# Gate and up projections with stationary weights in the four feed-forward blocks of a two-layer trunk

## Chip, cores and metric

The kernel runs on one core of a Trainium2 chip. The metric is the device time of one execution in microseconds (us). Before the change three runs took 990.55, 991.48 and 993.41 us; their median is 991.48 us.

## What is computed

The input is one sequence of 256 tokens with 1024 features, in float32. Two layers follow. Each layer has three residual steps, and each step ends in a layer norm: a feed-forward block (FFN), a mixer, and a second FFN. The mixer of layer 0 is attention beside a gated unit, that of layer 1 a matrix memory. Here is the part that the change touches:

```python
D_MODEL = 1024; SEQ = 256; D_FF = 2816

def swiglu(x, w_gu, w_down):
    g, u = jnp.split(x @ w_gu, 2, axis=-1)
    return (jax.nn.silu(g) * u) @ w_down

for l in range(DEPTH):
    x = layer_norm(ALPHA * x + 0.5 * swiglu(x, ffn_w_gu[l, 0], ffn_w_down[l, 0]), ...)
    ...  # mixer of the layer, then layer_norm
    x = layer_norm(ALPHA * x + 0.5 * swiglu(x, ffn_w_gu[l, 1], ffn_w_down[l, 1]), ...)
```

So there are four FFNs, each with a gate/up weight of 1024 x 5632 and a down weight of 2816 x 1024.

## The kernel before

**Numbers in two halves.** Every float32 operand of a large product is split into a high part (a cast to fp32r on ScalarE, line 92) and a rest (a subtraction on VectorE, line 93). A product is then three matmuls, `mm3` at lines 119 to 122: high by high, high by low, low by high, all added up in one PSUM tile.

**Weights.** All weights lie in one DRAM tensor `W` of pages of 128 x 1024 floats (512 KB), in the order of use. A page passes through three rings: raw (6 buffers, the DMA's target, `w_dma`, line 73), then `whi` and `wlo` (9 buffers each, written by `w_split`, line 78). When the last matmul on page n has been written down, `w_done(n)` (line 86) splits page n + 9 and loads page n + 15. The split of page n + 9 writes the buffers of page n, so it waits for the matmuls that read page n.

**x transposed.** `xTh` and `xTl` hold the two halves of x with the features on the partitions, 8 blocks of 128 features by 256 tokens. Each layer norm rewrites them, one half of the tokens (t = 0, 1) after the other.

**Two ways to project.** `proj` (line 241) keeps 128 tokens of x stationary and streams weights: four pages, eight blocks of features, three matmuls each, so 24 matmuls with a moving operand of 512 columns. Its output has tokens on the partitions. `proj_t` (line 255) keeps 128 x 128 weights stationary and streams x: one page, eight blocks, 24 matmuls with a moving operand of 256 columns (all tokens). Its output has features on the partitions, that is, it comes out transposed. Before the change only the mixers use `proj_t`, for 4 pages in layer 0 and 8 in layer 1.

**The FFN** (`ffn`, line 310). The 2816 hidden features are 11 groups of 256. One group takes four pages, in which 256 columns of gate stand beside 256 columns of up. For each group and each t, `proj` fills one PSUM bank (`bank_m`, 3 buffers) with gate in its first half and up in its second. Then `post` (line 313) does silu of the gate on ScalarE (line 315), times up on VectorE (line 316), two TensorE transposes into the bank `ps_t` (line 320), and a split of the result into the two halves of `hT` (lines 92 and 93). That is 22 such steps in an FFN and 88 in all. The down projection (`out_proj`, line 265) takes `hT` as its stationary operand, 22 blocks of 128 hidden features.

**What sets the order.** `post` is a generator. `tick()` (line 107), called between pieces of a projection, advances it, so that its transposes stand in the source some 18 matmuls after the projection that it belongs to. Line 36 has a manual schedule for SyncE (the queue of DMA issues) alone. On TensorE, ScalarE, VectorE and GpSimd the order of the source is a priority: the scheduler that lays out the program may put a later instruction first where the earlier one is not ready by its reckoning. The order on each engine is then fixed, and engines wait for one another by semaphores.

Of the kernel before, what the change touches and what calls it, by code (L numbers as in the profile page):

```python
# [7 lines left out]
F32 = mybir.dt.float32  # L8
F32R = mybir.dt.float32r
BF = mybir.dt.bfloat16  # L10
AF = mybir.ActivationFunctionType
OP = mybir.AluOpType
AX = mybir.AxisListType

P = 128
S = 256
# [3 lines left out]
FG = 11  # L20
FC = 22
# [9 lines left out]
def trunk(ctx, tc, W, xT_d, x_d, g_d, b_d, rope_d, id_d, idb_d, mk_d, tri_d, sel_d,  # L31
          sg_d, sb_d, sw_d, sbt_d, cw_d, wif_d, bif_d, hg_d, out_d):
    nc = tc.nc
# [5 lines left out]
    pages = ctx.enter_context(tc.tile_pool(name="pages", bufs=PAGES))  # L39
# [11 lines left out]
    def bank_m(shape=(P, 512)):  # L51
        return bank("m", 3, shape)

    def bank_t(shape=(P, 512)):
        return bank("t", 1, shape)

    def page(name, shape, dt=F32):
        n = 1
        for d in shape[1:]:
            n *= d  # L60
        v = pages.tile([P, 516], dt, tag="p2", name=name, bufs=PAGES)[:, 0:n]
        if len(shape) == 3:
            v = v.rearrange("p (a b) -> p a b", a=shape[1])
        elif len(shape) == 4:
            v = v.rearrange("p (a b c) -> p a b c", a=shape[1], b=shape[2])
        return v
# [24 lines left out]
    def split(src, hi, lo):  # L91
        nc.scalar.copy(out=hi, in_=src)  # L92
        nc.vector.tensor_tensor(out=lo, in0=src, in1=hi.bitcast(F32), op=OP.subtract)  # L93
# [3 lines left out]
    def spawn(gen):  # L97
        side.append([0, gen])
        return gen
# [13 lines left out]
    def finish(gen):  # L113
        for e in list(side):
            if e[1] is gen:
                while e in side:
                    step(e)
# [51 lines left out]
    for c in range(4):  # L169
        if c == 0:  # L170
# [3 lines left out]
            for i in range(2):  # L174
                w = slice(i * 512, (i + 1) * 512)
# [14 lines left out]
    def load_consts():  # L190
        nc.sync.dma_start(out=identb, in_=idb_d)
        nc.sync.dma_start(out=maskb, in_=mk_d)
        nc.sync.dma_start(out=tri, in_=tri_d)
        nc.sync.dma_start(out=sel, in_=sel_d)
        nc.sync.dma_start(out=cw, in_=cw_d)
        nc.sync.dma_start(out=bif, in_=bif_d)
# [44 lines left out]
    def proj(t, n0, release, out=None, js=range(4)):  # L241
        ps = out if out is not None else bank_m()
        for j in js:
            rh = whi[n0 + j].rearrange("p (a n) -> p a n", a=2)
            rl = wlo[n0 + j].rearrange("p (a n) -> p a n", a=2)
            for i in range(2):
                kc = 2 * j + i
                mm3(ps, xTh[:, kc, t * P:(t + 1) * P], xTl[:, kc, t * P:(t + 1) * P],
                    rh[:, i, :], rl[:, i, :], kc == 0, kc == 7)
            if release:  # L250
                w_done(n0 + j)
            tick()
        return ps
# [55 lines left out]

    def ffn(n0, k, ln_prev, last=False):  # L310
        hT = {}

        def post(g, t, ps):
            hp = pages.tile([P, 2, 256], F32, tag="h", name="hp", bufs=3)
            nc.scalar.activation(out=hp[:, 0, :], in_=ps[:, 0:256], func=AF.Silu)  # L315
            nc.vector.tensor_tensor(out=hp[:, 1, :], in0=hp[:, 0, :], in1=ps[:, 256:512], op=OP.mult)  # L316
            yield 2
            pt = bank_t((P, 2, P))
            for c in range(2):
                nc.tensor.transpose(pt[:, c, :], hp[:, 1, c * P:(c + 1) * P], ident)  # L320
            q = page("hT", [P, 2, 2, P], F32R)
            hT[g, t] = q
            split(pt, q[:, 0], q[:, 1])

        if ln_prev is None:
            load_consts()
        order = [(0, 0), (1, 0), (0, 1), (1, 1)] + [(g, t) for g in range(2, FG) for t in range(2)]
        gens = []
        if ln_prev is None:
            order = [(g, t) for g in range(1, FG) for t in range(2)]  # L330
            ps = [bank_m(), bank_m()]
            for j in range(4):
                proj(0, n0, False, ps[0], (j,))
                proj(1, n0, True, ps[1], (j,))
            for t in range(2):
                gens.append(spawn(post(0, t, ps[t])))
        for g, t in order:
            if (g, t) == (0, 1) and ln_prev is not None:
                finish(ln_prev)
            ps = proj(t, n0 + 4 * g, t == 1)  # L340
            gens.append(spawn(post(g, t, ps)))

        def lhs(c, t):
            if (c // 2, t) not in hT:
                for e in gens:
                    finish(e)
            q = hT[c // 2, t]
            return q[:, 0, c % 2, :], q[:, 1, c % 2, :]

        return out_proj(FC, n0 + 4 * FG, lhs, 7, k, 2.0 * ALPHA, 4.0 * EPS, last)  # L350

    def mixer_ab(n0, k, ln_prev):
# [173 lines left out]
    def mixer_c(n0, k, ln_prev):  # L526
# [196 lines left out]
        return out_proj(8, n0 + 24, lhs, 8, k, ALPHA, EPS, False)  # L723

    ln = ffn(0, 0, None)
    ln = mixer_ab(66, 1, ln)
    ln = ffn(94, 2, ln)
    ln = ffn(160, 3, ln)
    ln = mixer_c(226, 4, ln)
    ln = ffn(258, 5, ln, True)  # L730
# [3 lines left out]
def _arrays(np, i):  # L734
    f32 = np.float32
    import ml_dtypes
    c = np.ascontiguousarray
    parts = []

    def ffn(l, f):  # L740
        gu = i["ffn_w_gu"][l, f].reshape(4, 2, P, 2, FG, 256).transpose(4, 0, 2, 1, 3, 5)
        parts.append(gu.reshape(44, P, 1024))
        parts.append(i["ffn_w_down"][l, f].reshape(FC, P, 1024))

    def cols(w):
        g = w.shape[1] // 512
        return w.reshape(4, 2, P, g, 512).transpose(3, 0, 2, 1, 4).reshape(4 * g, P, 1024)

    def chunks(w):
        n = w.shape[1] // P  # L750
        return w.reshape(8, P, n, P).transpose(2, 1, 0, 3).reshape(n, P, 1024)

    ffn(0, 0)
    ab = i["ab_w_in"][0]
    parts.append(cols(ab[:, 0:1536]))
    parts.append(cols(ab[:, 2048:2560]))
    parts.append(chunks(ab[:, 1536:2048]))
    parts.append(i["ab_w_out"][0].reshape(8, P, 1024))
    ffn(0, 1)
    ffn(1, 0)  # L760
    cw = i["c_w_in"][0]
    parts.append(cols(cw[:, 2048:3072]))
    qk = [h + 4 * j for h in range(4) for j in range(2)]
    cqk, co_ = chunks(cw[:, 0:1024])[qk], cols(cw[:, 1024:2048])
    for g in range(2):
        parts.append(cqk[4 * g:4 * g + 4])
        parts.append(co_[4 * g:4 * g + 4])
    parts.append(i["c_w_out"][0].reshape(8, P, 1024))
    ffn(1, 1)
    a = {}  # L770
    a["W"] = np.concatenate(parts, axis=0)
    x = i["x"][0]
    a["xT"] = c(x.T.reshape(8, P, S).transpose(1, 0, 2))
    a["x"] = c(x.reshape(2, P, D).transpose(1, 0, 2))
    a["g"] = i["ln_g"].reshape(6, D)
    a["b"] = i["ln_b"].reshape(6, D)
    inv = (10000.0 ** (-(np.arange(32, dtype=f32) / f32(32)).astype(np.float64))).astype(f32)
    ang = (np.arange(S, dtype=f32)[:, None] * inv[None, :]).astype(np.float64)
    co, si = np.cos(ang), np.sin(ang)
    cs = np.concatenate([co, co], axis=1)  # L780
    sn = np.concatenate([-si, si], axis=1)
    r = np.stack([cs / 8, sn / 8, cs, sn], axis=1).astype(f32)
    a["rope"] = c(r.reshape(2, P, 4, 64).transpose(1, 0, 2, 3))
    a["id"] = np.eye(P, dtype=f32)
    a["idb"] = np.eye(P).astype(ml_dtypes.bfloat16)
    m = np.where(np.arange(P)[None, :] > np.arange(P)[:, None], -1e30, 0.0)
    a["mk"] = np.stack([m, m.T], axis=1).astype(ml_dtypes.bfloat16)
    a["tri"] = (np.arange(S)[None, :] >= np.arange(P)[:, None]).astype(f32)
    sel = np.zeros((P, 4, P), f32)
    for h in range(4):  # L790
        sel[h, h, :] = sel[32 + h, h, :] = -1.0
    a["sel"] = sel
    a["sg"] = i["sgu_ln_g"]
    a["sb"] = i["sgu_ln_b"]
    a["sw"] = c(i["sgu_w"][0].transpose(2, 0, 1))
    a["sbt"] = c(np.repeat(i["sgu_b"][0].reshape(4, 2, 1, P), 64, axis=2).reshape(4, P, P).transpose(1, 0, 2))
    cv = np.concatenate([i["c_conv_w"][0], i["c_conv_b"]], axis=0).reshape(5, 8, P)[:, qk]
    a["cw"] = c(cv.transpose(2, 1, 0))
    a["wif"] = c(cw[:, 3072:3080].reshape(8, P, 8).transpose(1, 0, 2).reshape(P, 64))
    a["bif"] = np.concatenate([i["c_b_i"], i["c_b_f"]], axis=1).reshape(8, 1)  # L800
    a["hg"] = i["c_head_g"]
    return a
# [23 lines left out]
```

## Time and profile before

| | |
|---|---|
| three runs, us | 990.55, 991.48, 993.41 |
| span of the profiled execution, first to last instruction | 987.7 us |
| TensorE (PE) busy | 974.8 us, 99% |
| weight loads (PEld) busy | 788.2 us, 80% |
| VectorE (DVE) busy | 599.0 us, 61% |
| ScalarE (ACT) busy | 463.2 us, 47% |
| mean granted TensorE clock | 0.999 |
| DMA, over the span | 185 GB/s mean, 330 GB/s in the first 25 us |

The profile gives the span of the one profiled execution; its own time is not listed beside those of the three runs. From the span to the median run there are 3.8 us, which lie before the first and after the last instruction or in the difference between executions.

In the rows below a time at the start of a line is that of the first instruction of the row, in us from the start of the span, and the next number is how long it was busy. "out<-in" are the program's names. For a matmul the first name after the arrow is the operand that streams, the second the stationary one, and the last number of the shape is the count of columns streamed. Matmuls overlap, so what a matmul costs is read from the distance between two starts, not from its duration.

### The profile page before, as it was taken

To read this page: it belongs to the slowest core of one execution; us is meant where nothing else is said; L and a number is where in the kernel's file an instruction comes from. 1 tells how busy PE (TensorE), PEld (TensorE's weight loads), DVE (VectorE), ACT (ScalarE), POOL (GpSimd) and SP (SyncE) were. 2 spreads that over 40 slices of the span, in tenths; PEclk is the share of its full clock that TensorE was granted. 3 is DMA by queue.
4 is the path that set the end of the run, shared out by engine and by line. 5 is a ranking of instruction groups with operands and counts; after the bars stand their busy time and mean duration, and the time that the engine had idled before them with its cause. 6 is when DMAs were issued, how large, how long until landed. Compare 5 with 4: busy or idle time off the path is not lost.

```text
span 987.7 us, 12215 instructions
## 1 busy us (share of the span) xinstructions
PE 974.8 (99%) x4584; PEld 788.2 (80%) x4584; DVE 599.0 (61%) x822; ACT 463.2 (47%) x664; POOL 25.3 (3%) x36
## 2 busy tenths in 40 slices
PE   8999999999999999999999999999999999999997
PEld 5888888887888888888888888888888788888886
DVE  6565554586768555554765555448767885555534
ACT  5454443346645444443354444324675444444420
POOL 0000000020100000000000000001000000000000
PEclk9999999999999999999999999999999999999999
DMA  8874465485336555555564455656633365555511
GB/s 330 296 270 171 171 213 192 132 284 180 117 124 232 193 187 186 196 186 188 177 217 172 170 173 190 213 172 213 214 125 123 133 216 207 184 196 182 192 43 43
DMA packets 52202, 182.81 MB, mean 185 GB/s; under 512 B 6192, under 2 KB 6832, under 8 KB 52016
## 3 DMA queue, kind: packets, MB, share of 16 engines
q1 hardware_dynamic: 52144, 182.04, 53.8%
q8 instruction: 36, 0.59, 0.2%
q14 instruction: 22, 0.18, 0.1%
HBM read 180.97 MB, written 1.05 MB: 184 GB/s over the span
## 4 chain that ended last, share of the span: by engine, by line
PE 70%; DVE 2%; POOL 0%; issue 0%; ACT 0%; DVEq 0%
PE ps_m L120 15%; PE ps_m L121 15%; PE ps_m L122 15%; PE ps_a L120 8%; PE ps_a L121 8%; PE ps_a L122 7%; PE ps_t L320 1%; DVE wlo L93 1%; PE ps_a L232 1%; POOL hrs L201 0%; ACT whi L92 0%; PE ps_a L471 0%; DVE hst L652 0%; DVE num L679 0%; PE ps_a L633 0%
## 5 line engine op out<-in xcount | busy, mean ns | idle before, releaser
L93 DVE TENSOR_TENSOR wlo<-raw,whi 128x1024 fp32r<-128x1024 f32 (+1 forms) x325 | 394.1, 1221 | 188.2 <-ACT whi L92 184.6
L92 ACT CAST whi<-raw 128x1024 fp32r<-128x1024 f32 (+1 forms) x325 | 339.6, 1049 | 251.9 <-PE ps_a L122 146.1
L120 PE MATMUL ps_m<-whi,xTh 128*128 128x512 f32 x832 | 338.0, 407 | 1.5 <-ACT whi L92 1.5
L121 PE MATMUL ps_m<-wlo,xTh 128*128 128x512 f32 x832 | 330.0, 397 | 0.5 <-DVE wlo L93 0.5
L122 PE MATMUL ps_m<-whi,xTl 128*128 128x512 f32 x832 | 329.2, 396 | 0.0
L122 PEld LDWEIGHTS ps_m<-whi,xTl 128*128 128x128 f32 x832 | 156.4, 188 | 37.2
L120 PEld LDWEIGHTS ps_m<-whi,xTh 128*128 128x128 f32 x832 | 156.6, 188 | 35.6 <-ACT whi L92 2.7
L121 PEld LDWEIGHTS ps_m<-wlo,xTh 128*128 128x128 f32 x832 | 156.8, 188 | 34.1 <-DVE wlo L93 1.2
L120 PE MATMUL ps_a<-whi,hT 128*128 128x512 f32 (+1 forms) x352 | 138.6, 394 | 0.0
L121 PE MATMUL ps_a<-wlo,hT 128*128 128x512 f32 (+1 forms) x352 | 138.0, 392 | 0.0
L122 PE MATMUL ps_a<-whi,hT 128*128 128x512 f32 (+1 forms) x352 | 137.8, 392 | 0.0
L92 ACT CAST hT<-ps_t 128x256 fp32r<-128x256 f32 x88 | 32.5, 369 | 118.2 <-PE ps_t L320 118.2
L93 DVE TENSOR_TENSOR hT<-ps_t,hT 128x256 fp32r<-128x256 f32 x88 | 37.0, 421 | 79.2 <-ACT hT L92 79.2
L122 PEld LDWEIGHTS ps_a<-whi,hT 128*128 128x128 f32 x352 | 66.1, 188 | 15.3
L120 PEld LDWEIGHTS ps_a<-whi,hT 128*128 128x128 f32 x352 | 66.1, 188 | 15.0
L121 PEld LDWEIGHTS ps_a<-wlo,hT 128*128 128x128 f32 x352 | 66.2, 188 | 14.9
L316 DVE TENSOR_TENSOR hp<-hp,ps_m 128x256 f32<-128x256 f32 x88 | 36.8, 418 | 38.4 <-ACT hp L315 38.4
L315 ACT ACTIVATE hp<-ps_m 128x256 f32<-128x256 f32 x88 | 33.5, 381 | 54.3 <-PE ps_m L122 53.9
L210 DVE SCALAR_TENSOR_TENSOR xn<-xn,ps_a 128x512 f32<-128x512 f32 x24 | 16.0, 684 | 37.1 <-PE ps_a L122 37.0
L320 PEld LDWEIGHTS ps_t<-ident,hp 128*128 128x128 f32 x176 | 24.3, 139 | 11.9
L320 PE MATMUL ps_t<-ident,hp 128*128 128x128 f32 x176 | 33.4, 271 | 0.0
L201 POOL TENSOR_TENSOR lnrs<-lnrs,half 128x1 f32<-128x1 f32 x12 | 11.4, 951 | 821.1 <-DVE lnrs L200 793.7
(185 smaller groups left out, 589.6 us busy)
## 6 DMA issues: line engine op xcount, KB each, us to landing
raw<-in_W SPq DMA_DIRECT2D x323, 512.0 KB, 4.3
gb<-in_g SPq DMA_DIRECT2D x6, 512.0 KB, 3.9
gb<-in_b SPq DMA_DIRECT2D x6, 512.0 KB, 4.6
xn<-in_x SPq DMA_DIRECT2D x1, 1024.0 KB
out<-xn SPq DMA_DIRECT2D x4, 256.0 KB, 2.3
xt<-in_xT SPq DMA_DIRECT2D x3, 256.0 KB, 6.2
raw<-in_W SPq DMA_DIRECT2D x2, 256.0 KB, 3.4
swt<-in_sw SPq DMA_DIRECT2D x2, 256.0 KB, 6.4
```

Of the source, the lines that this page charges most:

```text
L92: nc.scalar.copy(out=hi, in_=src)
L93: nc.vector.tensor_tensor(out=lo, in0=src, in1=hi.bitcast(F32), op=OP.subtract)
L120: mm_(out=out, lhsT=lh, rhs=rh, start=start, stop=False)
L121: mm_(out=out, lhsT=lh, rhs=rl, start=False, stop=False)
L122: mm_(out=out, lhsT=ll, rhs=rh, start=False, stop=stop)
L201: nc.gpsimd.tensor_tensor(out=r, in0=r, in1=half[:, :width], op=OP.pow)
L210: nc.vector.scalar_tensor_tensor(out=sl, in0=sl, scalar=scale, in1=acc[i], op0=OP.mult, op1=OP.add)
L232: nc.tensor.transpose(pt[:, c, :], sl[:, c * P:(c + 1) * P], ident)
L315: nc.scalar.activation(out=hp[:, 0, :], in_=ps[:, 0:256], func=AF.Silu)
L316: nc.vector.tensor_tensor(out=hp[:, 1, :], in0=hp[:, 0, :], in1=ps[:, 256:512], op=OP.mult)
L320: nc.tensor.transpose(pt[:, c, :], hp[:, 1, c * P:(c + 1) * P], ident)
```

## The change

`ffn` gets a parameter `head`: 1 for the first FFN of the program, 2 for the other three. The first `head` groups of 256 hidden features are projected as before, with `proj` and `post`. The other hidden features are taken in chunks of 128 by a new function `chunk`: 20 chunks in the first FFN and 18 in each of the others, 74 in all. A chunk takes two pages, one of gate and one of up. `proj_t` of the gate page writes the first half of a bank, silu reads that half, `proj_t` of the up page writes the second half of the same bank, VectorE multiplies, and the product is split into `hT` from SBUF. There are no TensorE transposes in a chunk, and nothing in it is a generator: its instructions are written down at once. On the host the pages of the chunks are laid out as `proj_t` wants them. The number and size of the pages stay.

```diff
     def ffn(n0, k, ln_prev, last=False):
         hT = {}
+        head = 1 if ln_prev is None else 2
...
             q = page("hT", [P, 2, 2, P], F32R)
-            hT[g, t] = q
+            for c in range(2):
+                hT[2 * g + c, t] = (q[:, 0, c, :], q[:, 1, c, :])
             split(pt, q[:, 0], q[:, 1])
+
+        def chunk(c):
+            n = n0 + 4 * head + 2 * (c - 2 * head)
+            ps = bank_m()
+            hp = pages.tile([P, 2, 256], F32, tag="h", name="hp", bufs=3)
+            proj_t(n, ps[:, 0:256])
+            nc.scalar.activation(out=hp[:, 0, :], in_=ps[:, 0:256], func=AF.Silu)
+            proj_t(n + 1, ps[:, 256:512])
+            nc.vector.tensor_tensor(out=hp[:, 1, :], in0=hp[:, 0, :], in1=ps[:, 256:512], op=OP.mult)
+            q = page("hT", [P, 2, S], F32R)
+            split(hp[:, 1, :], q[:, 0], q[:, 1])
+            for t in range(2):
+                w = slice(t * P, (t + 1) * P)
+                hT[c, t] = (q[:, 0, w], q[:, 1, w])
...
-        order = [(0, 0), (1, 0), (0, 1), (1, 1)] + [(g, t) for g in range(2, FG) for t in range(2)]
         gens = []
         if ln_prev is None:
-            order = [(g, t) for g in range(1, FG) for t in range(2)]
+            order = []
...
+        else:
+            order = [(0, 0), (1, 0), (0, 1), (1, 1)]
         for g, t in order:
...
+        for c in range(2 * head, FC):
+            chunk(c)
 
         def lhs(c, t):
-            if (c // 2, t) not in hT:
+            if (c, t) not in hT:
                 for e in gens:
                     finish(e)
-            q = hT[c // 2, t]
-            return q[:, 0, c % 2, :], q[:, 1, c % 2, :]
+            return hT[c, t]
...
-    def ffn(l, f):
-        gu = i["ffn_w_gu"][l, f].reshape(4, 2, P, 2, FG, 256).transpose(4, 0, 2, 1, 3, 5)
-        parts.append(gu.reshape(44, P, 1024))
+    def ffn(l, f, head):
+        w = i["ffn_w_gu"][l, f]
+        gu = w.reshape(4, 2, P, 2, FG, 256).transpose(4, 0, 2, 1, 3, 5)
+        parts.append(gu[0:head].reshape(4 * head, P, 1024))
+        gc = w.reshape(8, P, 2, FC, P).transpose(3, 2, 1, 0, 4)
+        parts.append(gc[2 * head:].reshape(2 * (FC - 2 * head), P, 1024))
         parts.append(i["ffn_w_down"][l, f].reshape(FC, P, 1024))
...
```

## Rows read from the trace of the kernel before

**Rows 1.** The page, part 1: busy time, share of the span, instructions

```profile
PE 974.8 (99%) x4584; PEld 788.2 (80%) x4584; DVE 599.0 (61%) x822; ACT 463.2 (47%) x664; POOL 25.3 (3%) x36
```

**Rows 2.** PE's waits, longest in total: us in total, times, longest

```profile
PE ps_m L120 <- ACT whi L92: 1.5, 1, 1.5
PE ps_m L120 <- DVE qkc L619: 1.4, 1, 1.4
```

**Rows 3.** Groups of instructions: xcount | busy us, mean ns | idle before, releaser

```profile
L320 PE MATMUL ps_t<-ident,hp 128*128 128x128 f32 x176 | 33.4, 271 | 0.0
L92 ACT CAST whi<-raw 128x1024 fp32r<-128x1024 f32 x323 | 338.4, 1052 | 250.5 <-PE ps_a L122 146.1 <-PE ps_m L122 89.9 <-PE ps_m L121 8.6
L93 DVE TENSOR_TENSOR wlo<-raw,whi 128x1024 fp32r<-128x1024 f32 x323 | 392.8, 1224 | 186.6 <-ACT whi L92 183.1 <-DMA raw<-in_W 0.2
L315 ACT ACTIVATE hp<-ps_m 128x256 f32<-128x256 f32 x88 | 33.5, 381 | 54.3 <-PE ps_m L122 53.9
L316 DVE TENSOR_TENSOR hp<-hp,ps_m 128x256 f32<-128x256 f32 x88 | 36.8, 418 | 38.4 <-ACT hp L315 38.4
L92 ACT CAST hT<-ps_t 128x256 fp32r<-128x256 f32 x88 | 32.5, 369 | 118.2 <-PE ps_t L320 118.2
L93 DVE TENSOR_TENSOR hT<-ps_t,hT 128x256 fp32r<-128x256 f32 x88 | 37.0, 421 | 79.2 <-ACT hT L92 79.2
```

**Rows 4.** Timeline of PE, first FFN, one projection to the next

```profile
93.87 0.48 PE L120 MATMUL ps_m<-whi,xTh 128*128 128x512 f32 x1
94.19 0.40 PE L121 MATMUL ps_m<-wlo,xTh 128*128 128x512 f32 x1
...
99.56 0.38 PE L320 MATMUL ps_t<-ident,hp 128*128 128x128 f32 x2
99.69 0.48 PE L120 MATMUL ps_m<-whi,xTh 128*128 128x512 f32 x1
```

**Rows 5.** Timeline of PE, mixer of layer 0: matmuls of proj_t

```profile
265.84 0.28 PE L121 MATMUL ps_m<-xTl,whi 128*128 128x256 f32 x1
...
268.67 0.28 PE L121 MATMUL ps_m<-xTl,whi 128*128 128x256 f32 x1
...
270.24 0.28 PE L121 MATMUL ps_m<-xTl,whi 128*128 128x256 f32 x1
...
273.98 0.39 PE L120 MATMUL ps_a<-whi,cah 128*128 128x512 f32 x1
```

**Rows 6.** Timelines of PE and ACT, mixer of layer 1: one bank, two column ranges

```profile
723.68 0.23 PE L603 MATMUL ps_a<-maskb,identb 128*128 128x128 bf16 x1
...
723.87 0.23 PE L603 MATMUL ps_a<-maskb,identb 128*128 128x128 bf16 x1
...
724.14 0.47 ACT L606 ACTIVATE pT<-ps_a,cnat 128x256 f32<-128x256 f32 x1 [1.09 <-PE ps_a L603]
```

**Rows 7.** Timelines of PE and ACT, first FFN: end of a projection to its silu

```profile
101.17 0.40 PE L120 MATMUL ps_m<-whi,xTh 128*128 128x512 f32 x1
...
101.37 1.05 ACT L92 CAST whi<-raw 128x1024 fp32r<-128x1024 f32 x1 [0.30 <-PE ps_m L122]
102.33 0.38 ACT L315 ACTIVATE hp<-ps_m 128x256 f32<-128x256 f32 x1
```

**Rows 8.** Timeline of PE, mixer of layer 1: gates beside proj_t

```profile
707.59 0.28 PE L122 MATMUL ps_m<-xTh,wlo 128*128 128x256 f32 x1
707.79 0.28 PE L553 MATMUL ps_a<-ident,ifr 8*128 8x8 f32 x2
...
708.23 0.28 PE L121 MATMUL ps_m<-xTl,whi 128*128 128x256 f32 x1
...
713.24 0.28 PE L122 MATMUL ps_m<-xTh,wlo 128*128 128x256 f32 x1
713.81 0.60 PE L564 MATMUL ps_a<-tri,gnl 128*4 128x256 f32 x2 [0.29 <-DVE gnl L560]
```

**Rows 9.** Timeline of PE, mixer of layer 0: attention beside proj_t

```profile
261.59 0.36 PE L121 MATMUL ps_m<-xTl,whi 128*128 128x256 f32 x1
...
262.26 0.28 PE L120 MATMUL ps_m<-xTh,whi 128*128 128x256 f32 x1
262.51 0.66 PE L447 MATMUL ps_a<-ptp,vs 128*64 128x128 f32 x8
```

More of the change, by code (lines that the diff above doesn't have):

```diff
@@ L751, in chunks @@
         return w.reshape(8, P, n, P).transpose(2, 1, 0, 3).reshape(n, P, 1024)
-    ffn(0, 0)
+    ffn(0, 0, 1)
     ab = i["ab_w_in"][0]
@@ L758, in _arrays @@
     parts.append(i["ab_w_out"][0].reshape(8, P, 1024))
-    ffn(0, 1)
-    ffn(1, 0)
+    ffn(0, 1, 2)
+    ffn(1, 0, 2)
     cw = i["c_w_in"][0]
@@ L768, in _arrays @@
     parts.append(i["c_w_out"][0].reshape(8, P, 1024))
-    ffn(1, 1)
+    ffn(1, 1, 2)
     a = {}
```

## Prediction

> **What bounds the kernel now.** I read the page's first part first: TensorE (PE) is busy for 974.8 of 987.7 us, with the other engines at 61% and less [rows 1]. Then PE's own waits: the two longest are 1.5 and 1.4 us, in an execution of almost a millisecond [rows 2]. So time goes down only if PE gets less to do, and up whenever PE is made to wait. Last I read PE's timeline, because matmuls overlap and their cost is the distance between starts. In the FFN, one projection of 24 matmuls and the two transposes that come with it take 5.82 us, from 93.87 to 99.69 [rows 4]. Within it the 23 matmuls from 94.19 to 99.56 stand 233.5 ns apart [rows 4].
>
> **What is removed.** 24 x 0.2335 us are 5.60 us, so two transposes cost 5.82 - 5.60 = 0.22 us of PE. (Their durations say 271 ns each [rows 3]; overlap makes that useless here.) Before there are 88 such pairs. The first FFN keeps 2 and the others 4 each, so 74 go: 74 x 0.216 = **16.0 us less**.
>
> **What is exchanged.** 74 x 24 = 1776 matmuls of 512 columns become 3552 of 256 columns. The mixers already run `proj_t`, so the price is in the trace: 32 of them from 270.24 to 273.98, 116.9 ns each [rows 5]. Two make 233.8 ns against 233.5: 1776 x 0.3 ns = **0.5 us more**. The bounds come from two other stretches. 43 spacings from 708.23 to 713.24 give 116.5 ns, so 0.9 us less [rows 8]; 24 from 265.84 to 268.67 give 117.9 ns, so 4.1 us more [rows 5]. I take 116.9 because it is the longest stretch with no other work in between that ends on a clean border. Weight loads double in number, one for each half-length matmul, and stay hidden as they do in those same rows. The Trainium skill, page "TensorE: Matmul & The Clock Gate", section "Back-to-back issue gap", has 262 cycles for 256 columns and 518 for 512: two halves cost 6 cycles more than a whole. By that the exchange would cost 4.4 us (an estimate, 1776 x 6 cycles at 2.4 GHz) and the sum would end 3.9 us higher; the stretches measured here lie mostly below it, so the measurement decides.
>
> **What moves, and what covers it.** Silu, product and split have the same count and shape as before: 88 of each. Per chunk, ACT has two weight casts, a silu and a cast of `hT`: 2 x 1.05 + 0.38 + 0.37 = 2.85 us. DVE has 2 x 1.22 + 0.42 + 0.42 = 3.29 us [rows 3]. Both fit into the 48 matmuls of a chunk, 5.61 us. If that cover failed, the bank would come free late; there are three, so only a delay of a whole chunk would reach PE. The pages keep number and size: one DMA issue for each page on SP's queue, in the same order. What changes is the rhythm. Before, four pages are freed in 5.6 us and none in the next 5.6 us; now one every 2.8 us. That is no more pressing than before, and PE waited for weights only once, at the start [rows 2], in the first group, which the change leaves as it is. I cost this at nothing.
>
> **The new wait.** Within a chunk the up matmuls write the second half of a bank while silu still has to read the first half. The columns do not overlap. Does PE have to wait for silu? The nearest row is an exp on ACT that reads columns 0 to 255 of a bank of which PE then writes columns 256 to 383. The matmul that completes the first range began at 723.68 and ran 0.23 us; the one that completes the second began at 723.87 and ended at 724.10. The exp, with ACT idle for 1.09 us before it, began at 724.14 [rows 6]. It waited for the other columns of its bank. So I expect the same in the other direction: the first up matmul waits for silu.
>
> The price if PE just stood there: in the FFN now, the projection before 101.17 is followed on ACT by the cast of a page that it freed (101.37, 1.05 us) and then by its silu, which ends at 102.33 + 0.38 = 102.71 [rows 7]. The next matmul could have begun at 101.17. So 1.54 us for each chunk, 74 x 1.54 = 114 us.
>
> But PE's order is not that of the source. In the source, the matmuls of line 564 stand 24 `proj_t` matmuls after those of line 553; on the chip 45 stand between them, up to 713.24 [rows 8]. The scheduler found line 564 not ready and took matmuls of the next projection, into the next bank, first. A chunk offers the same way out: the next chunk's gate page has 24 matmuls for another bank, its weights are split many pages ahead, and 1.54 us need only 13 of them (1.54 / 0.117). I expect gate matmuls of chunk c + 1 in front of the up matmuls of chunk c.
>
> What is left is the error of that reckoning: the order is fixed, and if silu ends later on the chip than reckoned, PE stands. Two rows show such a place. At 262.51, after six `proj_t` matmuls that filled the time [rows 9], PE's step is 0.25 us, against 0.20 us for a change of operation that waits for nothing (707.59 to 707.79 [rows 8]): about 0.04 us lost. At 713.81 the step is 0.57 us: 0.36 us lost [rows 8]. The first waits for one ACT instruction, as a chunk would; the second for a chain of small ones on two engines. I take 0.04 us, nearest in kind: 74 x 0.04 = **3.0 us more**, with the bounds nothing and 74 x 0.36 = 26.6 us.
>
> **The sum.** -16.0 + 0.5 + 3.0 = -12.5 us. It was made on the profiled execution, span 987.7 us; the median of the runs is 3.8 us above that, and nothing in the change touches what lies around the span. 991.5 - 12.5 = **979 us**.
>
> **Rivals.**
> - *Nothing is left of the wait.* The reckoning may be late rather than early, or the hold on the bank may not apply to a write after a read. Then only the first two terms stand: 991.5 - 15.5 = 976 us. For it: PE waits almost nowhere in the whole trace [rows 2], though much of its order is laid out this way. Against it: rows 6.
> - *The wait is filled, but badly.* One mechanism: PE's queue holds the first up matmul until silu is done, and the weight cast ahead of silu on ACT makes silu late by the same amount in every chunk. It decides from 15.5 / 74 = 0.21 us a chunk. At the 0.36 us of rows 8 the time is 991.5 - 15.5 + 26.6 = 1003 us, slower than before. For it: a bias repeats 74 times, and does not average out. Against it: rows 9, and that PE has the next matmuls at hand.
> - *Half of that.* 0.17 to 0.25 us a chunk, and the change pays for itself and no more: 988.5 to 994.5 us.
> - *No fill at all.* PE runs each chunk in the order of the source: 991.5 - 15.5 + 114 = 1090 us. The Trainium skill speaks for it: page "PSUM — Partial Sum Buffer", section "PSUM bank collisions raise a hardware error", has the rule that semaphores are to guard a bank (by quadrant), not an address. By that rule the up matmuls of a chunk and the silu of its gate cannot overlap; rows 6 agree with it, and rows 8 show that PE can do other work meanwhile.
> - *The change does not do what it says*, in that loading a new weight for each 256 columns is what binds. Excluded: rows 5 and 8 already show that rate with a new weight for each matmul.
>
> **How the numbers follow.** Forecast 0.40, with its own range from 976 to 986 us (a wait of 0 to 0.13 us a chunk). No wait left 0.27. Half 0.13. Filled badly 0.14. No fill 0.06. About 0.3%, or 3 us, is what a measurement of this kernel can tell from no change. So faster has 0.40 + 0.27 = 0.67, same 0.13, slower 0.20. The range goes from 974 (no wait, the lower bound of the exchange, a microsecond of spread between runs) up to 1000, which takes in the middle case and the milder part of the bad fill. It leaves out the worse part and the case without fill, somewhat over one in ten.
>
> **What would show it.** In the profile of the changed kernel: 28 transposes of line 320's kind instead of 176; matmuls of chunks some 117 ns apart; on PE's timeline in each chunk 24 gate matmuls, about 13 of the next chunk's gate, then the up matmuls; a list of PE's waits with "ps_m <- ACT hp" of some 3 us or a gap just too short to be listed; and the four FFNs shorter by about 3 us each, the mixers unchanged. If the gate and up matmuls stand in the order of the source with holes of 1.5 us, the forecast is wrong by that step. If the spacing in the chunks is 118 ns or more, the exchange was mis-sized: each further nanosecond is 3.6 us.

## The result, and the profile after

Four runs of the changed kernel have a median of 998.38 us (997.64 to 998.46). Four runs of the kernel before on the same chip have 991.47 us. The ratio is 1.0069 [1.0055 to 1.0084]: **slower by 6.9 us**, or 0.7%, where 12.5 us less were forecast. 998.38 us lies near the upper end of the range, but on the other side of no change.

The profiled execution took 998.46 us, its span is 996.5 us. The page of the changed kernel, part 1:

```profile
span 996.5 us, 15539 instructions
PE 981.1 (98%) x6212; PEld 863.5 (87%) x6212; DVE 596.0 (60%) x822; ACT 458.4 (46%) x664; POOL 23.8 (2%) x36
```

Against [rows 1], PE has 1628 instructions more: 1776 more matmuls and 148 fewer transposes. It is still called busy for 98% of the span. By the groups of instructions the edit did what it says:

```profile
L120 PE MATMUL ps_m<-xTh,whi 128*128 128x256 f32 x1280 | 366.4, 286 | 3.1 <-DVE qkc L637 1.4
...
L321 PE MATMUL ps_t<-ident,hp 128*128 128x128 f32 x28 | 5.5, 278 | 0.0
L332 ACT ACTIVATE hp<-ps_m 128x256 f32<-128x256 f32 x74 | 27.9, 378 | 6.4 <-PE ps_m L122 6.4
```

28 transposes are left of 176 [rows 3], and the 74 chunk silus take as long as before. So where is the time? PE's list of waits names nothing that the FFNs do:

```profile
PE ps_m L120 <- ACT whi L92: 2.5, 1, 2.5
PE ps_m L120 <- DVE qkc L637: 1.4, 1, 1.4
```

The list of the weight loads' waits (engine PEld; us in total, times, longest) does:

```profile
PEld ps_m L120 <- ACT hp L332: 16.2, 69, 0.4
PEld ps_m L120 <- ACT whi L92: 3.8, 3, 2.9
```

Sixty-nine times the weight load of a chunk's first up matmul waited for silu (line 332). On PE itself the hole is hidden, because a matmul is shown busy for 0.28 us and the next normally starts 0.117 us after it: a step that comes up to 0.16 us late still leaves PE "busy" throughout. One chunk on PE's timeline (start, us busy, engine, line):

```profile
400.63 0.39 PE L120 MATMUL ps_m<-xTh,whi 128*128 128x256 f32 x1
...
404.94 0.28 PE L122 MATMUL ps_m<-xTh,wlo 128*128 128x256 f32 x1
405.06 0.28 PE L120 MATMUL ps_m<-xTh,whi 128*128 128x256 f32 x1
...
406.22 0.28 PE L121 MATMUL ps_m<-xTl,whi 128*128 128x256 f32 x1
406.52 0.38 PE L120 MATMUL ps_m<-xTh,whi 128*128 128x256 f32 x1
406.75 0.28 PE L121 MATMUL ps_m<-xTl,whi 128*128 128x256 f32 x1
406.86 0.28 PE L122 MATMUL ps_m<-xTh,wlo 128*128 128x256 f32 x1
```

and the same stretch on ACT:

```profile
405.14 1.06 ACT L92 CAST whi<-raw 128x1024 fp32r<-128x1024 f32 x1 [0.16 <-PE ps_m L121]
406.09 0.38 ACT L332 ACTIVATE hp<-ps_m 128x256 f32<-128x256 f32 x1
```

The gate's last matmul starts at 404.94. From 405.06 to 406.22 PE takes 11 matmuls of the next chunk's gate. The first up matmul starts at 406.52, 0.30 us after the last of these, not 0.117. Behind it the next step is 0.23 us (406.52 to 406.75), and then the pace is normal again (406.75 to 406.86). ACT does the weight cast first and silu from 406.09 to 406.47. The up matmul follows silu's end by 0.05 us.

I counted every place where PE's step is too long in this way, from the starts on its timeline: 75 places (3 of them in the mixers, also there before). The first up matmul is late by 0.162 us in the mean and the matmul behind it by 0.112 us. Together 0.27 us a place, 20.5 us in all.

One stretch differs for another reason. The windows of the first 10 to 25 us (us, busy and count for PE, PEld, DVE, ACT and POOL, granted clock, DMA share, GB/s), first of the changed kernel, then of the kernel before:

```profile
10.00:25.00 15.00, 12.81 (x58) 10.43 (x59) 10.79 (x12) 8.93 (x11) 0.00 (x0) 0.89 0.91 347
```

```profile
10.00:25.00 15.00, 14.29 (x61) 11.26 (x62) 12.01 (x13) 9.87 (x14) 0.00 (x0) 1.00 1.01 390
```

In this one execution PE waited 2.5 us for a page of its first group (before 1.5 us [rows 2]). Soon after, for some 3 us, its 512-column matmuls came 0.43 us apart instead of 0.233, and the mean granted clock of the stretch is 0.89. The first group, which the change does not touch, ends about 3 us later, at 22.5 us instead of 19.5. This start varies between executions (in the profiled runs of the experiments the first chunks begin between 20.9 and 23.9 us), so the spans differ by 8.8 us where the medians differ by 6.9. I use medians for totals and stretches inside the FFNs for causes.

### The profile page after: what moved, and what is told of

The parts are those of the page before. It is cut to its first block, busy times and chain, and to the rows that moved or that the text cites. A ratio compares the mean times of both kernels' runs of the same rounds, so it can differ in the third digit from the quotient of the medians.

```text
span 996.5 us, 15539 instructions
## 1 busy us (share of the span) xinstructions
PE 981.1 (98%) x6212; PEld 863.5 (87%) x6212; DVE 596.0 (60%) x822; ACT 458.4 (46%) x664; POOL 23.8 (2%) x36
## 4 chain that ended last, share of the span: by engine, by line
PE 94%; DVE 2%; issue 1%; ACT 1%; DMA 1%; POOL 0%; SPq 0%; DVEq 0%; ACTq 0%
PE ps_m L120 22%; PE ps_m L121 20%; PE ps_m L122 20%; PE ps_a L121 10%; PE ps_a L120 9%; PE ps_a L122 9%; DVE wlo L93 1%; PE ps_a L232 1%; DMA raw<-in_W 1%; PE ps_a L428 1%; POOL hrs L201 0%; ACT whi L92 0%; PE ps_a L465 0%; PE ps_t L321 0%; ACT hp L332 0%
## 5 line engine op out<-in xcount | busy, mean ns | idle before, releaser
L120 PE MATMUL ps_m<-xTh,whi 128*128 128x256 f32 x1280 | 366.4, 286 | 3.1 <-DVE qkc L637 1.4
L121 PE MATMUL ps_m<-xTl,whi 128*128 128x256 f32 x1280 | 357.6, 280 | 0.0
L122 PE MATMUL ps_m<-xTh,wlo 128*128 128x256 f32 x1280 | 347.2, 279 | 0.0
L120 PEld LDWEIGHTS ps_m<-xTh,whi 128*128 128x128 f32 x1280 | 240.4, 188 | 18.6 <-ACT hp L332 16.2
L121 PEld LDWEIGHTS ps_m<-xTl,whi 128*128 128x128 f32 x1280 | 240.7, 188 | 0.4 <-issue 0.2
L122 PEld LDWEIGHTS ps_m<-xTh,wlo 128*128 128x128 f32 x1280 | 236.3, 188 | 0.3 <-issue 0.3
L120 PE MATMUL ps_m<-whi,xTh 128*128 128x512 f32 x240 | 98.3, 411 | 2.6 <-ACT whi L92 2.5
L121 PE MATMUL ps_m<-wlo,xTh 128*128 128x512 f32 x240 | 96.7, 403 | 0.5 <-DVE wlo L93 0.5
L122 PE MATMUL ps_m<-whi,xTl 128*128 128x512 f32 x240 | 95.9, 400 | 0.0
L121 PEld LDWEIGHTS ps_m<-wlo,xTh 128*128 128x128 f32 x240 | 45.9, 191 | 10.8 <-DVE wlo L93 1.2
```

Of the source, the lines that this page charges most:

```text
L120: mm_(out=out, lhsT=lh, rhs=rh, start=start, stop=False)
L121: mm_(out=out, lhsT=lh, rhs=rl, start=False, stop=False)
L122: mm_(out=out, lhsT=ll, rhs=rh, start=False, stop=stop)
```

## The experiments

Theory A: the up matmuls wait for silu because both use one bank, the matmuls that the scheduler puts between are too few, and 74 times some 0.27 us is lost. Rival B: 256-column matmuls with stationary weights are dearer than [rows 5] said, or something else in the new form costs the time. All edits are made to the changed kernel.

**Two banks.** Gate and up get a PSUM tile and a bank each; nothing else differs in the source.

```diff
-            ps = bank_m()
+            pg, pu = bank_m((P, S)), bank_m((P, S))
...
-            proj_t(n, ps[:, 0:256])
+            proj_t(n, pg)
...
-            proj_t(n + 1, ps[:, 256:512])
+            proj_t(n + 1, pu)
```

> Gate and up of a chunk go to two banks of 256 columns instead of the two halves of one. Theory A (the bank holds the up matmuls until silu has read the gate): in the changed kernel 75 places cost 0.162 us of standing and 0.112 us at the matmul behind it, 20.5 us in all; without the shared bank they go, so 998.4 - 20.5 = 978 us, and no step on PE's timeline within the chunks ends on a silu. Theory B (the loss belongs to the rhythm of the chunks themselves, that is to switching from one accumulation to another or to the pages that are freed, and not to the bank): the holes stay and the time is 998 us.

Measured: 975.80 us against 990.51, ratio 0.9847 [0.983 to 0.9863]. Its list of the weight loads' waits has no silu left, and no hole remains in its chunks (PE's timeline below it):

```profile
PEld ps_m L120 <- ACT whi L92: 3.5, 3, 2.4
PEld L145 <- issue: 2.0, 7, 0.3
PEld L431 <- issue: 1.9, 7, 0.3
PEld ps_m L120 <- ACT cch L92: 1.6, 1, 1.6
```

```profile
400.22 0.28 PE L120 MATMUL ps_m<-xTh,whi 128*128 128x256 f32 x1
...
405.82 0.28 PE L120 MATMUL ps_m<-xTh,whi 128*128 128x256 f32 x1
```

48 matmuls from 400.22 to 405.82 are 5.60 us, 116.7 ns each. In the changed kernel the same 48 took 5.89 us (400.63 to 406.52). So the form of the projection costs what was forecast, and the loss hangs on the shared bank. Two things are not separated by this run. Without the wait PE need not mix two accumulations either, so the mixing could be to blame; the runs with no fill and with 15 ahead, below, settle that against B. And each half now has a tile as well as a bank of its own, so whether the program orders the two by tile or by bank was not tried. This version beats both kernels, by 14.7 us and 22.6 us.

**Gate one chunk ahead.** The bank stays shared, but a whole gate projection of the next chunk stands in the source between a chunk's gate and its up.

```diff
-        for c in range(2 * head, FC):
-            chunk(c)
+        gate(2 * head)
+        for c in range(2 * head, FC):
+            if c + 1 < FC:
+                gate(c + 1)
+            chunk(c)
```

`gate(c)` is the first half of the old `chunk` up to silu, `chunk(c)` the rest; the pages are laid out in that order.

> The bank is shared as in the changed kernel, but the source (and the order of the pages) has the gate of chunk c + 1 ahead of the up of chunk c, so 24 matmuls or 2.8 us lie between a gate and its up. Theory A: silu, 1.5 us behind the gate, is always done by then, so nothing waits: 978 us, as with two banks. A variant of A, that a matmul with a wait on ACT costs 0.11 us even where the wait is long over: 998.4 - 75 x 0.162 = 986 us. Theory B: 998 us.

Measured: 976.80 us, ratio 0.9858 [0.9843 to 0.9873]. The longest of the weight loads' waits is at the start, and silu is not in the list:

```profile
PEld ps_m L120 <- ACT whi L92: 4.5, 3, 2.5
```

The shared bank costs nothing that these runs can tell (976.8 us against 975.8, with ranges that overlap) when 24 matmuls stand between. So it is not sharing as such, but the time that PE has to fill.

**Silu ahead of the cast, first try.** `proj_t` writes silu down before it calls `w_done`.

```diff
+            if read is not None:
+                read()
...
-            proj_t(n, ps[:, 0:256])
-            nc.scalar.activation(out=hp[:, 0, :], in_=ps[:, 0:256], func=AF.Silu)
+            proj_t(n, ps[:, 0:256],
+                   lambda: nc.scalar.activation(out=hp[:, 0, :], in_=ps[:, 0:256], func=AF.Silu))
```

> Silu of the gate is written down ahead of the split of the page that the gate has freed, so ACT does it first. Theory A, with the cast of 1.05 us ahead of silu as the part that the scheduler reckons too short: silu ends some 0.5 us behind the gate, the scheduler fills four or five matmuls, the standing time of 0.162 us falls to under 0.05 us, and the 0.112 us at the second matmul stay: 998.4 - 75 x 0.12 = 989 to 990 us. If the miss is the same for each wait, whatever stands ahead of silu: 998 us. Theory B: 998 us.

Measured: 997.96 us, ratio 1.0073 [1.0058 to 1.0088]. This decided nothing, since ACT's order did not change:

```profile
404.68 1.05 ACT L92 CAST whi<-raw 128x1024 fp32r<-128x1024 f32 x1 [0.16 <-PE ps_m L121]
405.64 0.37 ACT L334 ACTIVATE hp<-ps_m 128x256 f32<-128x256 f32 x1
```

The last reader of `whi` is the high-by-low matmul of line 121, one before the last (line 122), so the cast can start a matmul earlier than silu, and the scheduler lets it.

**No fill.** A chunk's gate is tied behind the last up matmul of the chunk before.

```diff
-            proj_t(n, ps[:, 0:256])
+            if ups:
+                with tc.issue_after(ups[-1].ins):
+                    proj_t(n, ps[:, 0:256])
+            else:
+                proj_t(n, ps[:, 0:256])
...
-            proj_t(n + 1, ps[:, 256:512])
+            ups.append(proj_t(n + 1, ps[:, 256:512]))
```

> The changed kernel, with the first gate matmuls of a chunk tied behind the up matmuls of the chunk before, so that PE keeps the order of the source. It prices what the filling hides. Theory A: PE stands from the end of each gate to the end of its silu, 1.5 us, where it now loses 0.27 us; about 70 places x 1.35 us more, 998.4 + 95 = 1090 to 1095 us. If the wait is not what rules, or is hidden in another way: near 998 us.

Measured: 1066.01 us, ratio 1.076 [1.0738 to 1.0781]. PE's list of waits, and one place on its timeline:

```profile
PE ps_m L120 <- ACT hp L339: 69.7, 58, 1.3
```

```profile
610.27 0.28 PE L122 MATMUL ps_m<-xTh,wlo 128*128 128x256 f32 x1
611.85 0.39 PE L120 MATMUL ps_m<-xTh,whi 128*128 128x256 f32 x1 [1.30 <-ACT hp L339]
```

The step is 1.58 us, 1.46 more than the normal 0.117, where 1.54 were worked out from [rows 7]. The total is below what was expected because only 58 of the 74 chunks stood, nine of them (the first of each FFN and five more at the start of the program) for less than 1.46 us. In the last four chunks of each FFN the scheduler filled with matmuls of the down projection, which were not tied. By the starts on the timeline the 58 first steps are too long by 79 us together, the steps behind them by 6 us (0.11 each) and the 16 filled places by 3 us. These 88 us on top of the two-bank kernel's 975.8 give 1064, against 1066.0 measured. Nothing is mixed in the chunks that stood, and they lose the most: it is the wait, not the mixing, that costs.

**Silu ahead of the cast, enforced.** As the first try, with the cast tied behind silu.

```diff
-            w_done(n)
+            with tc.issue_after(read().ins):
+                w_done(n)
```

> The changed kernel with the cast of the freed page tied behind silu on ACT (in the run with silu written down first, ACT still did the cast first, since the cast becomes ready one matmul earlier). Silu should end 0.5 us behind the gate instead of 1.5 us. If what the scheduler reckons too short is the cast, the standing time of 0.16 us a chunk goes and only the 0.11 us at the second matmul stay: 998.4 - 75 x 0.16 = 986 us, 990 at most. If the shortfall is the same for each wait, however long the wait: 998 us. By the shared bank alone (theory A) both are possible, but not 978.

Measured: 1000.15 us, ratio 1.0092 [1.0077 to 1.0107]. ACT and PE in the same stretch, and the weight loads' wait:

```profile
405.95 0.38 ACT L336 ACTIVATE hp<-ps_m 128x256 f32<-128x256 f32 x1 [1.16 <-PE ps_m L122]
406.23 1.04 ACT L92 CAST whi<-raw 128x1024 fp32r<-128x1024 f32 x1
```

```profile
405.57 0.28 PE L122 MATMUL ps_m<-xTh,wlo 128*128 128x256 f32 x1
405.69 0.28 PE L120 MATMUL ps_m<-xTh,whi 128*128 128x256 f32 x1
...
405.93 0.28 PE L122 MATMUL ps_m<-xTh,wlo 128*128 128x256 f32 x1
406.04 0.74 PE L120 MATMUL ps_m<-xTh,whi 128*128 128x256 f32 x2
406.61 0.28 PE L121 MATMUL ps_m<-xTl,whi 128*128 128x256 f32 x1
```

```profile
PEld ps_m L120 <- ACT hp L336: 18.6, 69, 0.3
```

Now silu starts 0.38 us behind the start of the gate's last matmul, where it was 1.15 us. The scheduler cut the fill to 4 matmuls to match (the row at 406.04, x2, joins the fourth with the first up matmul), and the first up matmul was late by 0.23 us, the one behind it by 0.105 us. So the cast, though it delays silu, is not what makes the fill too short. Whether silu ends 1.4 us behind the gate or 0.6, the fill falls short by about the same amount.

**Twelve and fifteen ahead.** If the fill is merely too short, more matmuls of the next gate, forced in front of up, should recover the time step by step.

```diff
+            if c + 1 < FC:
+                ahead[c + 1] = bank_m()
+                proj_t(n + 2, ahead[c + 1][:, 0:256], range(4))
             proj_t(n + 1, ps[:, 256:512])
```

`range(4)` gives 4 x 3 = 12 matmuls, `range(5)` 15; the next chunk does the other blocks of its gate.

> Shared bank. The source puts 12 of the 24 gate matmuls of chunk c + 1 ahead of the up matmuls of chunk c; the scheduler of the changed kernel put 11 there. If the loss is the missing part of a wait of 1.51 us behind the gate (12 x 0.117 = 1.40 us), 0.05 to 0.1 us of standing and the 0.11 us at the second matmul stay in 74 places: 978 + 74 x 0.16 to 0.21 = 990 to 994 us. If the loss had nothing to do with how many matmuls lie between: 998 us.

> The same with 15 gate matmuls ahead, 15 x 0.117 = 1.76 us, more than the 1.51 us that silu takes to end. If the loss is the missing part of the wait, and the 0.11 us at the second matmul only come where PE has to stand, both go: 976 to 978 us. If the 0.11 us belong to each matmul that is tied to ACT by a wait: 986 us. If the number of matmuls between does not matter: 998 us.

Measured: with 12, 987.82 us, ratio 0.9975 [0.9964 to 0.9985]; with 15, 980.65 us, ratio 0.9895 [0.9879 to 0.9911]. PE at the hand-over, with 12 and then with 15:

```profile
406.17 0.28 PE L122 MATMUL ps_m<-xTh,wlo 128*128 128x256 f32 x1
406.35 0.38 PE L120 MATMUL ps_m<-xTh,whi 128*128 128x256 f32 x1
406.57 0.28 PE L121 MATMUL ps_m<-xTl,whi 128*128 128x256 f32 x1
```

```profile
23.89 0.28 PE L120 MATMUL ps_m<-xTh,whi 128*128 128x256 f32 x1
...
405.66 0.28 PE L122 MATMUL ps_m<-xTh,wlo 128*128 128x256 f32 x1
405.78 0.31 PE L120 MATMUL ps_m<-xTh,whi 128*128 128x256 f32 x1
405.93 0.28 PE L121 MATMUL ps_m<-xTl,whi 128*128 128x256 f32 x1
```

With 12 the first step is 0.18 us, 0.06 late, and the second 0.22, 0.10 late: one more matmul takes about 0.1 us off the first step and leaves the second. Added up from the starts on the timelines, the steps in the FFNs that are too long come to 20.6 us in the changed kernel and to 11.5 with 12 ahead: 9.1 us of the 10.6 between 998.4 and 987.8. The rest was not traced. With 15 the first step is normal and about 0.03 us or less is left at the second, in all but five places: the last chunk of each FFN, which has no next gate, and one chunk of the first FFN still lose 0.13 to 0.37 us. All this comes to 2.8 us, against 0.4 us in the two-bank kernel. PE mixes two accumulations here as in the change, and hardly loses by it. With 12 the time is better than expected by 2 us, with 15 worse by 3. The 2.4 us just named are a part of these; the profiled run with 15 also began its first chunk late, at 23.89 us (the first line of its fence), against 22.01 in the two-bank kernel, with a mean granted clock of 0.77 from 10 to 25 us against 0.89. Put in order, by the matmuls between the end of a gate and its up (the runs come from three sessions, in which the kernel before had 991.5, 990.5 and 990.2 us):

| matmuls between | time, us |
|---|---|
| none in 58 chunks (no fill) | 1066.0 |
| 11 (the change) | 998.4 |
| 12 | 987.8 |
| 15 | 980.7 |
| 24 (gate one chunk ahead) | 976.8 |
| own bank, no wait | 975.8 |

The kernel with the cast behind silu is not on this line, since its wait itself is shorter. One matmul more a chunk decides whether the change loses 0.7% or wins 0.2%.

## Why the prediction was wrong, point by point

**What bounds the kernel** held. PE stays the bound in every version, and all differences are counts and steps of PE.

**The 74 pairs of transposes** (-16.0 us) and **the exchange** (+0.5) were right. From the mean steps within the FFNs' projections (233.3 ns for 512 columns before, 2 x 116.7 ns in the two-bank kernel) the exchange costs 0.1 ns x 1776 = 0.2 us, inside its bounds. The estimate of 4.4 us, from the figures of the Trainium skill (page "TensorE: Matmul & The Clock Gate", section "Back-to-back issue gap"), is not what these runs show. -16.0 + 0.2 = -15.8; the two-bank kernel, which has these two terms and no wait, measured -14.7 between the medians. Its profiled execution is shorter by 13.4 us (974.3 against 987.7) although its first group ends 2.5 us later, so by 15.9 us behind that.

**The cover for ACT, DVE and pages** held: the two-bank kernel has the same work on all of them and loses nothing to them.

**That the up matmuls wait for silu** was right, and the two-bank kernel against the change shows it: the columns of gate and up do not overlap, and a bank of its own removes the wait. The rule of the Trainium skill that the prediction named (page "PSUM — Partial Sum Buffer", section "PSUM bank collisions raise a hardware error") agrees with these runs in what it asks for; no run here shows what happens without the semaphore. **The price without fill** was right as well, 1.46 us measured for 1.54. **That the scheduler fills** with the next chunk's gate was right; it put 11 matmuls there, 13 were forecast.

**The step that failed** is the next one: "What is left is the error of that reckoning", taken as 0.04 us a chunk. It measured 0.16 + 0.11 = 0.27 us, 20.5 us in all instead of 3.0. The reading of rows 9 went wrong. The step of 0.25 us there was compared with 0.20 us, a change of operation that "waits for nothing", and only the difference was booked. But in a chunk the last filler and the waiting matmul are of one kind, and the step to compare with is the normal 0.117 us. Against that step rows 9 show 0.13 us lost, nearly the 0.162 measured in the chunks. Why the scheduler's fill falls short by this much stays open. The second part, 0.11 us at the matmul behind the waiting one, I did not look for. It comes with the wait: it stands behind the late up matmuls in the change, in the no-fill kernel, with silu first and with 12 ahead, at 0.10 to 0.11 us whether the wait ahead was 0.06 or 1.46 us.

A likely source can be read from the weight loads of the chunk shown above:

```profile
406.11 0.19 PEld L121 LDWEIGHTS ps_m<-xTl,whi 128*128 128x128 f32 x1
406.52 0.19 PEld L120 LDWEIGHTS ps_m<-xTh,whi 128*128 128x128 f32 x1 [0.23 <-ACT hp L332]
406.63 0.19 PEld L121 LDWEIGHTS ps_m<-xTl,whi 128*128 128x128 f32 x1
406.75 0.19 PEld L122 LDWEIGHTS ps_m<-xTh,wlo 128*128 128x128 f32 x1
```

In the stream a load starts one step ahead of its matmul: the load at 406.11 belongs to the matmul at 406.22. The load at 406.52 is the one that waited for silu, and its matmul is shown from the same 406.52, busy for 0.38 us instead of 0.28. Its load lies beside nothing, and the matmul behind pays 0.11 us. It takes no hole to lose this. In a chunk of the first FFN the fill was just long enough, and the loss is there all the same:

```profile
61.49 0.28 PE L122 MATMUL ps_m<-xTh,wlo 128*128 128x256 f32 x1
61.60 0.39 PE L120 MATMUL ps_m<-xTh,whi 128*128 128x256 f32 x1
61.83 0.28 PE L121 MATMUL ps_m<-xTl,whi 128*128 128x256 f32 x1
61.95 0.28 PE L122 MATMUL ps_m<-xTh,wlo 128*128 128x256 f32 x1
```

```profile
61.16 0.39 ACT L332 ACTIVATE hp<-ps_m 128x256 f32<-128x256 f32 x1 [0.83 <-PE ps_m L122]
```

Silu ends at 61.55, the up matmul starts in its normal place at 61.60, and the next one comes 0.23 us later. That the missing look-ahead of the load is the reason is read from these rows; no run took it away by itself, but with 15 ahead, where silu is done earlier, 0.03 us of the 0.11 is left.

**The sum with the measured terms** for one FFN of 18 chunks: 18 x (-0.216 + 0.002 + 0.27) = +1.0 us, where 0.002 us is the exchange, 24 x 0.1 ns. In the three long FFNs most places lose 0.18 + 0.11 = 0.29 us, somewhat more than the mean; with that the sum is +1.4. From the last down matmul of the first FFN to that of the second, before took 289.39 us (197.45 to 486.84) and after 290.74 (201.94 to 492.68): +1.35 us. The two other long FFNs show +1.42 and +1.51. The two-bank kernel took 285.24 us (195.82 to 481.06), 4.15 less than before. For the whole kernel -16.0 + 0.2 + 20.6 = +4.8 us, with 20.6 us for all steps of the FFNs that are too long, without the three places in the mixers. The traces show more: the first FFN is longer by 1.5 us from the end of its first group on, so the four are longer by 5.8 us together, against 6.9 between the medians. What lies between 4.8 and 5.8 was not traced, and the last 1.1 us is less than the spread of before's own runs, 2.9.

**The rivals.** "Filled, but badly" was the right one: the place, and the point from which it decides, 0.21 us a chunk, held. It was priced at 0.36 us and measured 0.27, so 998 us and not 1003. Its cause did not hold: the cast ahead of silu is not what makes the fill short (the run with the cast behind silu). I gave it 0.14 because I took the shortfall for an error that averages out; the argument written beside it, that a bias repeats 74 times, should have had the weight. "Nothing left" describes the two-bank kernel, with a bank that the change does not have. "No fill" needed an order that had to be forced.

**The signs named.** 28 transposes and 117 ns a matmul were there. The wait on silu was there too, but at 16.2 us in the list of the weight loads, not some 3 us in PE's. The FFNs got 1.4 us longer, not 3 us shorter.

## What to carry to other kernels

When a hand-over from PE to another engine and back is filled with other matmuls, look at the step from the last filler to the first dependent matmul and at the one behind it, against the step of the undisturbed stream; a list of PE's waits can be empty while 2% of the time goes there. Count a price for every such hand-over whose fill may end just short, here 0.27 us, before weighing it against what the change removes, here 0.22 us. If banks are free, give the reader and the writer one each; if not, put clearly more matmuls between them than the wait is long.

## What was not expected of the hardware

- A matmul released by a semaphore just in time still costs its successor 0.10 to 0.11 us, about the 0.117 us of a whole 256-column matmul.
- The hand-over from PE to ACT and back was short of cover by about as much with 4 matmuls of fill (0.23 + 0.105 us) as with 11 (0.162 + 0.112 us). What the first part consists of, the signal to ACT, silu's own length or the signal back, was not tried.
- In the changed kernel's profiled run, a wait of 2.5 us in the first group was followed by 512-column matmuls 0.43 us apart instead of 0.233, with a mean granted clock of 0.89 from 10 to 25 us: for part of that stretch the clock was at its lower level. In the run of before, with a wait of 1.5 us, the same stretch has 1.00. The wait alone does not decide it: in the profiled run with 12 ahead it was 2.5 us too, and the stretch has 1.00. Why the page comes later in some executions stays open.
